# Inverting the scan's triangles by substitution on 16x16 blocks joined on TensorE, with two buffers for one stream of the preparation

## The chip, the cores and the metric

The kernel runs on one core of a Trainium2 chip. Times are device microseconds (us) of one execution. The metric is that time; lower is better. The engines are named as the profile names them: PE is TensorE, DVE is VectorE, ACT is ScalarE, POOL is GpSimd, SP is the engine that issues most of the loads.

## The reference

One layer of a bidirectional encoder, 1024 tokens of width 1024, all in float32: an FFN, a mixing layer (eight heads of banded attention beside eight heads of a two-way delta-rule scan), and a second FFN, each between norms and added to the stream. The change touches the scan alone:

```python
def _rwkv7_step(state, inp):
    r, w, k, v, kk, kka = inp
    sa = jnp.einsum('dbhvk,dbhk->dbhv', state, kk)
    state = state * w[..., None, :] - sa[..., :, None] * kka[..., None, :] + v[..., :, None] * k[..., None, :]
    y = jnp.einsum('dbhvk,dbhk->dbhv', state, r)
    return state, y
...
    _, ys = lax.scan(_rwkv7_step, state0, xs)      # 1024 steps, 2 directions, 8 heads of 64
    y = ys[:, :, 0] + jnp.flip(ys[:, :, 1], axis=1)
```

A step at a time would be 1024 steps in a row. The kernel computes 64 tokens (a chunk) at once. Within a chunk, each token's correction depends on those of the tokens before it, through a unit lower triangular 64x64 matrix, one for each chunk, direction and head. That matrix has to be inverted before the chunk's outputs and its final state can be had from matrix products.

## The kernel before

The program (`run`) goes through FFN 1, the input projection with the attention, the scan stage, the finish of the scan's output, the output projection and FFN 2. The scan stage takes 8 blocks of 2 chunks (`NB` = 8, `BLK` = 2, `C` = 64). One block has 2 chunks x 2 directions x 8 heads = 32 triangles. A block passes through four steps:

- `prep(n)` (L783) loads the block's streams for each direction: decay and rate (`th_w`, `th_a`, two buffers each) and one tile `in3` with r, k and kk (one buffer, so the second direction's load waits until the first direction's readers are through). DVE and ACT scale them, PE multiplies them (`lp`, L830), DVE masks the products into `lm` (L832), which holds the triangles. PE transposes `bk` into `bp` (L838). SP then writes the diagonal 32x32 blocks of `lm` to the scratch `x_d` in DRAM (4 DMAs, L846).
- `solve(n)` (L850) loads them back as `X`: 64 triangles of 32x32, each on two partitions that take alternate columns of the inverse. Two DVE operations a step (L866 multiplies, L868 subtracts) do the substitution in 31 steps into `Ti`. L870 copies `Ti` transposed, and POOL writes both to scratch (`t_d`, `tt_d`, 2 + 2 DMAs, L872 and L873).
- `merge(n)` (L875) loads the inverses of the diagonal blocks to where the products need them (`d11`, 2 DMAs, L883; `tt`, 4 DMAs, L886, all on POOL) and joins pairs of 32 to 64 by two products: `pa` (32 matmuls, L894), a copy on ACT (L896), `pb` (32 matmuls, L900), and a negated copy on ACT into `tt` (L902).
- `chain(n)` (L918) takes the block's two chunks in turn, each from the state `sv` that the one before left. PE: `xu` (L941); ACT copies it to `xs` (L944); PE: `xu` again, with the inverse `tt` as weights (L952, called the inverse product below); ACT copies to `uv`; PE: state and outputs `st`, `y` (L937, a helper's line); DVE scales the state into the next chunk's `sv` (L968).

Two more kinds of work lie between these on the same engines: the attended half of the output projection (`project_attended`: `po` L1064 and `yq` L1075 on PE, `yat` L1072 on DVE), which needs nothing of the scan, and the loads of `uv` and `sv` on POOL (`values`, L908).

What sets the order: the body of the loop calls merge(n), chain(n), and then prep and solve of block n+3, and a scheduler of the framework reorders the instructions of each engine by its own costs; on each engine they then run strictly in that order. Three sets of block buffers (`R0`, `R1`, `B0`) are used in turn, so prep(n+3) writes `lm` only where chain(n) has read it for the last time. A float32 matmul stands in the trace as two records, so 32 matmuls are 64 records.

Of the kernel before, what the change touches and what calls it, by code (L numbers as in the profile page):

```python
# [26 lines left out]
C, NC_, BLK = 64, 16, 2  # L27
TB = C * BLK
# [3 lines left out]
def _ap(src, off, pat):  # L32
    return bass.AP(tensor=src.tensor, offset=src.offset + off, ap=pat)
# [3 lines left out]
class _GateUp:  # L37
# [126 lines left out]
class _Kernel:  # L164
# [618 lines left out]
    def prep(self, n, p, psum, big):  # L783

        nc, V, A, T = self.nc, self.nc.vector, self.nc.scalar, self.nc.tensor
# [6 lines left out]
        for d in range(2):  # L792
# [48 lines left out]
            for k, v in (("pr", pt), ("bt", bt)):  # L841
                blk[k].append(v)
        for par in range(2):
            for k in range(2):
                r0 = par * 64 + k * 32
                self.nc.sync.dma_start(_ap(self.x_d[n % 4], (k * 2 + par) * 16 * 1024, [[32, 32], [1024, 16], [1, 32]]),  # L846
                                  lm[r0:r0 + 32, par, :, :, :, k * 32:k * 32 + 32].rearrange("p d i a t -> p (d i a) t"))
        return blk

    def solve(self, n, p):  # L850


        nc, V, G = self.nc, self.nc.vector, self.nc.gpsimd
        X = p.tile([128, 32, 32], F32, name="X", tag="X", bufs=2)
        for q in range(2):
            self.load(X[q * 64:q * 64 + 64].rearrange("p a b -> p (a b)"), self.x_d[n % 4])
        Ti = p.tile([128, 32, 16], F32, name="Ti", tag="Ti", bufs=2)
        tmp = p.tile([128, 144], F32, name="ttmp", tag="ttmp", bufs=2)
        tf = Ti.rearrange("p a b -> p (a b)")
        G.memset(tf, 0.0)  # L860
        for q in range(2):
            G.memset(tf[q * 64:q * 64 + 64, q * 16:512:33], 1.0)
        for s in range(31):
            r, m = 31 - s, s // 2 + 1
            tv = tmp[:, :r * m].rearrange("p (a b) -> p a b", a=r)
            V.tensor_tensor(tv, X[:, s, s + 1:][:, :, None].to_broadcast([128, r, m]),  # L866
                            Ti[:, s, 0:m][:, None, :].to_broadcast([128, r, m]), op=OP.mult)
            V.tensor_tensor(Ti[:, s + 1:, 0:m], Ti[:, s + 1:, 0:m], tv, op=OP.subtract)  # L868
        Tt = X[:, 0:16, :]
        V.tensor_copy(Tt, Ti.rearrange("p a b -> p b a"))  # L870
        for q in range(2):
            self.nc.gpsimd.dma_start(_ap(self.t_d[n % 4], q * 16, [[1024, 32], [32, 32], [1, 16]]), Ti[q * 64:q * 64 + 32])  # L872
            self.nc.gpsimd.dma_start(_ap(self.tt_d[n % 4], q * 32, [[1024, 64], [64, 16], [1, 32]]), Tt[q * 64:q * 64 + 64])  # L873

    def merge(self, n, blk, p, psum):  # L875

        nc, A, T = self.nc, self.nc.scalar, self.nc.tensor
# [3 lines left out]
        for par in range(2):  # L881
            o = par * 64
            self.nc.gpsimd.dma_start(d11[o:o + 32], _ap(self.t_d[n % 4], par * 16 * 1024, [[32, 32], [1024, 16], [1, 32]]))  # L883
            for k in range(2):
                r0 = o + k * 32
                self.nc.gpsimd.dma_start(tt[r0:r0 + 32, :, k * 32:k * 32 + 32],  # L886
                          _ap(self.tt_d[n % 4], (k * 2 + par) * 16 * 1024, [[32, 32], [1024, 16], [1, 32]]))
        pa = psum.tile([128, NI, 32], F32, name="pa", tag="mg")
        am = d11
# [5 lines left out]
        for lo, hi in lohi:  # L895
            A.copy(am[hi].rearrange("p i (c q) -> p i q c", q=2), pa[hi].rearrange("p i (q c) -> p i q c", q=2))  # L896
        pb = psum.tile([128, NI, 32], F32, name="pb", tag="mg")
# [201 lines left out]
    def constants(self):  # L1099
# [6 lines left out]
        for c, t in self.eps.items():  # L1106
# [16 lines left out]
        self.x_d, self.t_d, self.tt_d = ([self.dram(f"{n}{j}", [r, w]) for j in range(4)]  # L1123
                                         for n, r, w in (("x", 64, 1024), ("t", 32, 1024), ("tt", 64, 1024)))

# [31 lines left out]

    def scan_inverses(self, p):
        self.tt = [p.tile([128, 2 * BLK * 4, 64], F32, name=f"tt{j}") for j in range(2)]
        for t in self.tt:  # L1160
            self.nc.gpsimd.memset(t.rearrange("p a b -> p (a b)"), 0.0)

    def run(self):
        nc = self.nc
# [4 lines left out]
        with self.top as top:  # L1169
# [106 lines left out]
            self.scan_inverses(sc)  # L1276
            sc.tile([128, 112], F32, name="edge")
            s_eo, s_pe = ExitStack(), ExitStack()
# [157 lines left out]
```

## Time and profile before

| what | value |
|---|---|
| median of 3 runs | 2369.25 us (2357.99 to 2371.84) |
| the profiled execution's own time | 2369.46 us |
| its span in the trace | 2367.7 us |
| mean granted clock of TensorE in it | 0.96 |
| scan stage in it | about 1205 to 1590 us of the span |

How to read the rows further down. A row of the timeline has the start (us), the duration (us), the engine (an engine's name with a q is its DMA queue's issue), the line, the operation, output <- inputs, sizes, and how many records were drawn together; in brackets stands the idle time before it and what ended it. A row of groups has the count, then the busy time in us and the mean of one in ns, then the idle time ahead and its main causes. A row of stretches has start and end, length, then for PE, weight loads, DVE, ACT and POOL the busy us with the number of instructions, and last the granted clock of TensorE (1 is full), the busy share of the 16 DMA engines, and GB/s.

### The profile page before, as it was taken

Reading aid. Unit: us, or ns where it says so; the run is one execution under the profiler, and the core shown is the slowest. Engines: PE = TensorE matmul, PEld = TensorE weight load, DVE = VectorE, ACT = ScalarE, POOL = GpSimd, SP = SyncE. Lnnn points to the kernel's source line nnn. Section 1 sums busy time; section 2 is a strip of 40 time slices with the busy share of each in tenths; the row PEclk is TensorE's granted clock in tenths of the full one; section 3 lists DMA queues with packets and bytes.
Section 4 is the critical chain, followed back from the end, with each engine's and each line's share of the span. In section 5 each row is a group of like instructions: output and inputs, shape, how many; then the busy total and the mean of one; then the engine's idle time right before and its main releaser. Section 6 shows DMA issues by size and latency. Waiting matters only on the chain. (4 is left out here: it accounts for less than half of the span.)

```text
span 2367.7 us, 39507 instructions
## 1 busy us (share of the span) xinstructions
PE 2212.2 (93%) x14532; PEld 1784.9 (75%) x14532; DVE 1782.8 (75%) x2957; ACT 1034.4 (44%) x1958; POOL 608.7 (26%) x732
## 2 busy tenths in 40 slices
PE   6999999999999998999995889988799999999997
PEld 4788888878877676788774767765678888887886
DVE  8899999865676344667568767837889999987565
ACT  4322333354676413666545545445442333235453
POOL 6244443400000010111102242432334344441000
PEclk8999999999999998999996798989989999999999
DMA  5354445486652514322369676577534544447655
GB/s 156 107 174 151 170 146 170 167 266 193 220 185 98 193 42 134 91 81 71 94 161 223 165 183 176 151 208 256 178 95 168 174 167 154 169 153 265 195 188 181
DMA packets 359381, 386.04 MB, mean 163 GB/s; under 512 B 74258, under 2 KB 265618, under 8 KB 359188
## 3 DMA queue, kind: packets, MB, share of 16 engines
q1 hardware_dynamic: 308512, 276.43, 38.8%
q0 software_dynamic: 30320, 94.44, 11.3%
q10 hardware_dynamic: 20356, 12.66, 1.9%
q8 instruction: 114, 1.87, 0.3%
q14 instruction: 79, 0.65, 0.1%
HBM read 257.53 MB, written 125.89 MB: 162 GB/s over the span
## 5 line engine op out<-in xcount | busy, mean ns | idle before, releaser
L186 ACT ACTIVATE wh<-raw 128x512 fp32r<-128x512 f32 (+1 forms) x273 | 167.8, 626 | 264.1 <-DVE raw L62 95.0
L187 DVE TENSOR_TENSOR wl<-raw,wh 128x512 fp32r<-128x512 f32 (+1 forms) x273 | 277.6, 1020 | 3.1 <-ACT wh L186 2.0
L81 PE MATMUL gu<-xh,wh 128*128 128x512 f32 x704 | 277.9, 395 | 0.9 <-ACT xh L186 0.8
L81 PE MATMUL gu<-xl,wh 128*128 128x512 f32 x704 | 276.3, 393 | 0.0
L81 PE MATMUL gu<-xh,wl 128*128 128x512 f32 x704 | 276.2, 392 | 0.0
L415 PE MATMUL pd<-gl,gwh 128*128 128x512 f32 x616 | 240.4, 390 | 3.1 <-DVE gl L187 3.1
L415 PE MATMUL pd<-gh,gwh 128*128 128x512 f32 x616 | 239.6, 390 | 0.5 <-DVE row L86 0.5
L415 PE MATMUL pd<-gh,gwl 128*128 128x512 f32 x616 | 239.7, 389 | 0.0
L86 DVE TENSOR_TENSOR row<-gu,row 128x512 f32<-128x512 f32 x308 | 206.4, 682 | 23.2 <-PE gu L81 22.4
L187 DVE TENSOR_TENSOR gwl<-graw,gwh 128x512 fp32r<-128x512 f32 (+1 forms) x176 | 117.0, 667 | 129.7 <-ACT gwh L186 127.5
L116 POOL DMA_DIRECT2D d_hid<-row x154 | 84.7, 551 | 470.6 <-DVE row L114 444.2
L186 ACT ACTIVATE gwh<-graw 128x512 fp32r<-128x512 f32 (+1 forms) x176 | 101.4, 576 | 190.5 <-PE pd L415 162.2
L81 PEld LDWEIGHTS gu<-xh,wh 128*128 128x128 f32 x704 | 133.9, 190 | 29.5 <-ACT xh L186 2.0
L81 PEld LDWEIGHTS gu<-xl,wh 128*128 128x128 f32 x704 | 133.8, 190 | 27.9
L81 PEld LDWEIGHTS gu<-xh,wl 128*128 128x128 f32 x704 | 133.3, 189 | 27.5
L415 PEld LDWEIGHTS pd<-gl,gwh 128*128 128x128 f32 x616 | 115.6, 188 | 28.5 <-DVE gl L187 4.9
L415 PEld LDWEIGHTS pd<-gh,gwh 128*128 128x128 f32 x616 | 115.5, 188 | 25.6 <-DVE row L86 0.8
L415 PEld LDWEIGHTS pd<-gh,gwl 128*128 128x128 f32 x616 | 115.6, 188 | 23.8
L94 ACT ACTIVATE row<-row 128x512 f32<-128x512 f32 x44 | 27.9, 633 | 223.9 <-DVE row L86 216.4
L187 DVE TENSOR_TENSOR gl<-raw,gh 128x512 fp32r<-128x512 f32 x160 | 112.9, 717 | 15.7 <-ACT gh L186 15.4
L145 POOL TENSOR_TENSOR ws<-ws 128x512 f32<-128x512 f32 x88 | 114.4, 1300 | 1.2
L186 ACT ACTIVATE gh<-raw 128x512 fp32r<-128x512 f32 x160 | 98.0, 621 | 32.2 <-DMA raw<-in_ffn_w_down_dram 21.1
(356 smaller groups left out, 5353.4 us busy)
## 6 DMA issues: line engine op xcount, KB each, us to landing
d_hid<-row POOLq DMA_DIRECT2D x154, 256.0 KB, 2.5
graw<-d_hid SPq DMA_DIRECT2D x132, 256.0 KB, 3.0
raw<-in_ffn_w_gate_dram SPq DMA_DIRECT2D x88, 256.0 KB, 3.1
raw<-in_ffn_w_up_dram SPq DMA_DIRECT2D x88, 256.0 KB, 3.3
ws<-in_ffn_w_down_dram SPq DMA_DIRECT2D x88, 256.0 KB, 4.5
d_ws<-ws POOLq DMA_DIRECT2D x88, 256.0 KB, 2.3
raw<-d_ws SPq DMA_DIRECT2D x88, 256.0 KB, 2.7
raw<-in_ffn_w_down_dram SPq DMA_DIRECT2D x66, 256.0 KB, 3.3
```

The lines of the kernel that those rows point to most:

```text
L81: self.K.nc.tensor.matmul(ps, a[:, k, :], b[:, k, :], start=(k == 0 and i == 0), stop=(k == 3 and i == 2))
L86: add = lambda o, x: V.tensor_tensor(o, ps, x, op=OP.add)
L94: A.activation(y[:, 0], y[:, 0], AF.Silu)
L116: put = lambda n, y: G.dma_start(self.hid[n - 1, j // 2], y)
L145: G.tensor_tensor(o, a, b, op=OP.subtract)
L186: self.nc.scalar.activation(h, src, AF.Copy)
L187: (eng or self.nc.vector).tensor_tensor(l, src, h, op=OP.subtract)
L415: T.matmul(ps[x], a[:, ts], b, start=(m == 0 and k == 0), stop=(m == NM - 1 and k == 2))
```

## The change

Substitution now goes down to triangles of 16 only, and TensorE joins them to 32 before it joins 32 to 64 as before.

- `prep`: `in3` has two buffers. The diagonal blocks go to `x_d` as 16x16 blocks, in 8 DMAs.
- `solve`: one load. Each of the 128 partitions holds one whole 16x16 triangle (32 triangles x 4 diagonal blocks). 15 steps of two operations on at most 64 elements, one transposing copy of 256, and two contiguous writes.
- `merge`: 14 loads on POOL instead of 6, each 16 partitions x 16 x 16 (`tt` 8, `t0` 4, `d11` 2). New: product `p1` (64 matmuls of 32x32 weights and 16 columns), a copy on ACT that scales rows by -1 or 0 (`lower`), product `p2` (64 matmuls), product `p2b` for the transposed form (64 matmuls with 16-column weights), one DVE addition into `d11`, and 4 copies on ACT into `tt`. Then `pa` and `pb` as before. `d11`, `t0` and `p1` are now single tiles that last through the stage.
- once, in `scan_inverses`: clearing the new tiles and making `lower` with three small DVE operations.

```diff
-            x3 = p.tile([128, 3, 4, TB], F32, name="in3", tag="in3", bufs=1)
+            x3 = p.tile([128, 3, 4, TB], F32, name="in3", tag="in3", bufs=2)
...
-        for par in range(2):
-            for k in range(2):
-                r0 = par * 64 + k * 32
-                self.nc.sync.dma_start(_ap(self.x_d[n % 4], (k * 2 + par) * 16 * 1024, [[32, 32], [1024, 16], [1, 32]]),
-                                  lm[r0:r0 + 32, par, :, :, :, k * 32:k * 32 + 32].rearrange("p d i a t -> p (d i a) t"))
+        for q in range(8):
+            par, o = q // 4, q % 4 * 16
+            self.nc.sync.dma_start(_ap(self.x_d[n % 4], self.small(q), [[16, 16], [256, 16], [1, 16]]),
+                                   lm[par * 64 + o:par * 64 + o + 16, par, :, :, :, o:o + 16].rearrange(
+                                       "p d i a t -> p (d i a) t"))
...
+    def small(self, q):
+        return (q % 2 * 64 + q // 2 * 16) * 256
...
-        X = p.tile([128, 32, 32], F32, name="X", tag="X", bufs=2)
-        for q in range(2):
-            self.load(X[q * 64:q * 64 + 64].rearrange("p a b -> p (a b)"), self.x_d[n % 4])
+        X = p.tile([128, 16, 16], F32, name="X", tag="X", bufs=2)
+        self.load(X.rearrange("p a b -> p (a b)"), self.x_d[n % 4])
...
-        for s in range(31):
-            r, m = 31 - s, s // 2 + 1
+        for s in range(15):
+            r, m = 15 - s, s + 1
             tv = tmp[:, :r * m].rearrange("p (a b) -> p a b", a=r)
             V.tensor_tensor(tv, X[:, s, s + 1:][:, :, None].to_broadcast([128, r, m]),
                             Ti[:, s, 0:m][:, None, :].to_broadcast([128, r, m]), op=OP.mult)
             V.tensor_tensor(Ti[:, s + 1:, 0:m], Ti[:, s + 1:, 0:m], tv, op=OP.subtract)
...
-        for q in range(2):
-            self.nc.gpsimd.dma_start(_ap(self.t_d[n % 4], q * 16, [[1024, 32], [32, 32], [1, 16]]), Ti[q * 64:q * 64 + 32])
-            self.nc.gpsimd.dma_start(_ap(self.tt_d[n % 4], q * 32, [[1024, 64], [64, 16], [1, 32]]), Tt[q * 64:q * 64 + 64])
+        V.tensor_copy(X, Ti.rearrange("p a b -> p b a"))
+        self.nc.gpsimd.dma_start(self.t_d[n % 4], tf)
+        self.nc.gpsimd.dma_start(self.tt_d[n % 4], X.rearrange("p a b -> p (a b)"))
...
-        d11 = p.tile([128, NI, 32], F32, name="d11", tag="d11")
+        d11, t0, p1 = self.d11, self.t0, self.p1
...
+        block = lambda d, q: _ap(d[n % 4], self.small(q), [[16, 16], [256, 16], [1, 16]])
+        for q in range(8):
+            o = q * 16
+            if q % 2 == 0:
+                self.nc.gpsimd.dma_start(t0[o:o + 16], block(self.t_d, q))
+            elif q % 4 == 1:
+                self.nc.gpsimd.dma_start(d11[o:o + 16, :, 16:32], block(self.t_d, q))
+            c = o % 64
+            self.nc.gpsimd.dma_start(tt[o:o + 16, :, c:c + 16], block(self.tt_d, q))
+        quads = [(par, k, slice(par * 64 + k * 32, par * 64 + k * 32 + 32)) for k in range(2) for par in range(2)]
+        ps = psum.tile([128, NI, 16], F32, name="p1", tag="mg")
+        for j in range(NI):
+            d, i, pr = j // 8, j // 4 % 2, j % 4
+            for par, k, rs in quads:
+                T.matmul(ps[rs, j, :], lm[rs, par, d, i, pr, k * 32:k * 32 + 32], t0[rs, j, :], start=True, stop=True)
+        A.activation(p1, ps, AF.Copy, scale=self.lower)
+        ps = psum.tile([128, 2, NI, 16], F32, name="p2", tag="mg")
+        for j in range(NI):
+            for par, k, rs in quads:
+                T.matmul(ps[rs, 0, j, :], tt[rs, j, k * 32:k * 32 + 32], p1[rs, j, :], start=True, stop=True)
+        for j in range(NI):
+            for par, k, rs in quads:
+                T.matmul(ps[rs.start:rs.start + 16, 1, j, :], p1[rs, j, :], tt[rs, j, k * 32 + 16:k * 32 + 32],
+                         start=True, stop=True)
+        V.tensor_tensor(d11[:, :, 0:16], t0, ps[:, 0], op=OP.add)
+        for par, k, rs in quads:
+            o = rs.start
+            A.copy(tt[o:o + 16, :, k * 32 + 16:k * 32 + 32], ps[o:o + 16, 1])
```

Everything behind `pa` stays, 21 to 23 lines further down: in the changed kernel the operations of the substitution are L867 and L869, `p1` L895, `p2` L900, `p2b` L903, the addition L905, `pa` L915, `pb` L921, the state's scaling L989, the inverse product L973, `po` L1085.

The scheduler also orders the engines anew. On DVE, in the middle of the scan stage, the substitution of one block stood among the operations of the next block's prep (L810 to L832). `X`, `Ti` and `ttmp` are the tiles of solve, the tiles with `in_` are a direction's `in3`. Before:

```order
L866 TENSOR_TENSOR ttmp<-X,Ti 128x126
L868 TENSOR_TENSOR Ti<-Ti,ttmp 128x18x7
L1055 SCALAR_TENSOR_TENSOR wol<-wor,c_attn_out_g,woh 128x512
L866 TENSOR_TENSOR ttmp<-X,Ti 128x136
L832 TENSOR_TENSOR lm<-lp,k_tri 128x512
L868 TENSOR_TENSOR Ti<-Ti,ttmp 128x17x8
L832 TENSOR_TENSOR lm<-lp,k_tri 128x512
L866 TENSOR_TENSOR ttmp<-X,Ti 128x128
L832 TENSOR_TENSOR lm<-lp,k_tri 128x512
L868 TENSOR_TENSOR Ti<-Ti,ttmp 128x16x8
```

Now, in the same place (the substitution of block 2):

```order
L1093 TENSOR_TENSOR yat<-yat,rs 128x512
L867 TENSOR_TENSOR ttmp<-X,Ti 128x15
L869 TENSOR_TENSOR Ti<-Ti,ttmp 128x15
L867 TENSOR_TENSOR ttmp<-X,Ti 128x28
L869 TENSOR_TENSOR Ti<-Ti,ttmp 128x14x2
L867 TENSOR_TENSOR ttmp<-X,Ti 128x39
L869 TENSOR_TENSOR Ti<-Ti,ttmp 128x13x3
L867 TENSOR_TENSOR ttmp<-X,Ti 128x48
L869 TENSOR_TENSOR Ti<-Ti,ttmp 128x12x4
L867 TENSOR_TENSOR ttmp<-X,Ti 128x55
L869 TENSOR_TENSOR Ti<-Ti,ttmp 128x11x5
L905 TENSOR_TENSOR d_12027<-t_12028,p_13116 128x16x16
```

The substitution now runs in one piece, with the next blocks' preps ahead of it and behind it. The addition L905, the only DVE operation of a merge (here of block 0's), stands behind its sixth step.

On PE, around the merge of block 3, `pa` stood far ahead, and `pb` lay between the transposes of a prep. `lp` and `bp` belong to a prep, `xu`, `y` and `st` to the chain, `yq` and `po` to the output projection. Before:

```order
L830 MATMUL lp<-pr,bk 128x128 x16
L838 MATMUL bp<-ident,bk 128x64 x8
L900 MATMUL pb<-tt_12090,d_14043 32x32 x3
L838 MATMUL bp<-ident,bk 128x64 x8
L900 MATMUL pb<-tt_12090,d_14043 32x32 x29
L941 MATMUL xu<-sv,lm 64x64 x16
L937 MATMUL y<-pr,sv 64x64 x11
L952 MATMUL xu<-xs,tt_12090 64x64 x16
L1075 MATMUL yq<-ident,yat 128x128 x4
```

Now (`p_14496` is `p1`, `p_14562` holds `p2` and `p2b`):

```order
L838 MATMUL bp<-ident,bk 128x64 x8
L895 MATMUL p_14496<-t_12028,lm 32x16 x50
L958 MATMUL st<-sv,ident 64x256 x4
L958 MATMUL y<-pr,sv 64x64
L900 MATMUL p_14562<-p_12029,tt_12026 32x16 x64
L903 MATMUL p_14562<-tt_12026,p_12029 16x16 x64
L958 MATMUL y<-pr,sv 64x64 x15
L1096 MATMUL yq<-ident,yat 128x128 x4
L915 MATMUL pa<-d_12027,lm 32x32 x32
L962 MATMUL xu<-sv,lm 64x64
L1085 MATMUL po<-woh,yah 128x512
```

Both joins now stand behind the prep's products and in a row with the chain, with pieces of the chain (`st`, `y`) and of the output projection (`yq`, `po`) between one product and the next.

On POOL, the writes of block 3's substitution and the loads of its merge. Before:

```order
L872 DMA d_t_173<-Ti 1024x1x16
L873 DMA d_tt_185<-X 1024x1x32
L908 DMA sv<-d_vt 64x2x256 x2
L860 MEMSET Ti 128x512
L883 DMA d_14043<-d_t_173 32x16x32
L862 MEMSET Ti 64x16 x2
L886 DMA tt_12090<-d_tt_185 32x16x32 x2
L883 DMA d_14043<-d_t_173 32x16x32
L886 DMA tt_12090<-d_tt_185 32x16x32 x2
```

Now, directly behind the two writes L871 and L872:

```order
L929 DMA sv<-d_vt 64x2x256 x2
L862 MEMSET Ti 128x256
L863 MEMSET Ti 128x16
L929 DMA uv<-d_vt 64x2x256 x2
L888 DMA tt_12026<-d_tt_185 16x16x16 x2
L929 DMA sv<-d_vt 64x2x256 x2
L888 DMA tt_12026<-d_tt_185 16x16x16
L929 DMA uv<-d_vt 64x2x256 x2
L888 DMA tt_12026<-d_tt_185 16x16x16 x5
L884 DMA t_12028<-d_t_173 16x16x16 x3
L886 DMA d_12027<-d_t_173 16x16x16 x2
L884 DMA t_12028<-d_t_173 16x16x16
```

Ahead of the first list stands one more row of each write. There are now fewer writes and more loads, the loads of `uv` and `sv` lie among them, and the last load of `t0` stands behind the two of `d11`.

More of the change, by code (lines that the diff above doesn't have):

```diff
@@ L868, in solve @@
             V.tensor_tensor(Ti[:, s + 1:, 0:m], Ti[:, s + 1:, 0:m], tv, op=OP.subtract)
[L869 to L872, printed above, removed]
-            self.nc.gpsimd.dma_start(_ap(self.tt_d[n % 4], q * 32, [[1024, 64], [64, 16], [1, 32]]), Tt[q * 64:q * 64 + 64])
+        V.tensor_copy(X, Ti.rearrange("p a b -> p b a"))
@@ L875, in merge @@
+        self.nc.gpsimd.dma_start(self.t_d[n % 4], tf)
+        self.nc.gpsimd.dma_start(self.tt_d[n % 4], X.rearrange("p a b -> p (a b)"))
     def merge(self, n, blk, p, psum):
-        nc, A, T = self.nc, self.nc.scalar, self.nc.tensor
+        nc, A, V, T = self.nc, self.nc.scalar, self.nc.vector, self.nc.tensor
         NI, lm = 2 * BLK * 4, blk["lm"]
-        d11 = p.tile([128, NI, 32], F32, name="d11", tag="d11")
+        d11, t0, p1 = self.d11, self.t0, self.p1
         blk["tt"] = tt = self.tt[n % 2]
[L881 to L887, printed above, removed]
+        block = lambda d, q: _ap(d[n % 4], self.small(q), [[16, 16], [256, 16], [1, 16]])
@@ L895, in merge @@
         for lo, hi in lohi:
-            A.copy(am[hi].rearrange("p i (c q) -> p i q c", q=2), pa[hi].rearrange("p i (q c) -> p i q c", q=2))
+            A.copy(am[hi], pa[hi])
         pb = psum.tile([128, NI, 32], F32, name="pb", tag="mg")
@@ L1123, in constants @@
         self.x_d, self.t_d, self.tt_d = ([self.dram(f"{n}{j}", [r, w]) for j in range(4)]
-                                         for n, r, w in (("x", 64, 1024), ("t", 32, 1024), ("tt", 64, 1024)))
+                                         for n, r, w in (("x", 128, 256), ("t", 128, 256), ("tt", 128, 256)))
     def mix_columns(self):
@@ L1158, in scan_inverses @@
     def scan_inverses(self, p):
+        G, V = self.nc.gpsimd, self.nc.vector
         self.tt = [p.tile([128, 2 * BLK * 4, 64], F32, name=f"tt{j}") for j in range(2)]
-        for t in self.tt:
-            self.nc.gpsimd.memset(t.rearrange("p a b -> p (a b)"), 0.0)
+        self.d11 = p.tile([128, 2 * BLK * 4, 32], F32, name="d11")
+        self.t0, self.p1 = (p.tile([128, 2 * BLK * 4, 16], F32, name=n) for n in ("t0", "p1"))
+        for t in self.tt + [self.d11, self.t0]:
+            G.memset(t.rearrange("p a b -> p (a b)"), 0.0)
+        four = p.tile([128, 4], F32, name="four")
+        self.lower = p.tile([128, 1], F32, name="lower")
+        V.tensor_reduce(out=four, in_=self.ident.rearrange("p (a b c) -> p a b c", b=2, c=16)[:, :, 1], op=OP.add, axis=AX.X)
+        V.tensor_reduce(out=self.lower, in_=four, op=OP.add, axis=AX.X)
+        V.tensor_scalar(self.lower, self.lower, -1.0, None, op0=OP.mult)
     def run(self):
@@ L1276, in run @@
             self.scan_inverses(sc)
-            sc.tile([128, 112], F32, name="edge")
+            sc.tile([128, 96], F32, name="edge")
             s_eo, s_pe = ExitStack(), ExitStack()
```

6 lines of the change are left out of this document (3 added, 3 removed).

## The prediction

> **What bounds the kernel now.** I read the page's busy shares first, then the busy times by stretches of the scan stage, since the change touches nothing else, and then one line of the timeline that marks each block's progress. The page says PE first, DVE second:
>
> ```profile
> span 2367.7 us, 39507 instructions
> PE 2212.2 (93%) x14532; PEld 1784.9 (75%) x14532; DVE 1782.8 (75%) x2957; ACT 1034.4 (44%) x1958; POOL 608.7 (26%) x732
> ```
>
> That is an average over stages. The stretches are the start of the scan, the five block periods in which preps still run, and the two last blocks:
>
> ```profile
> 1205.00:1310.00 105.00, 76.90 (x637) 62.80 (x638) 80.29 (x210) 53.63 (x102) 17.24 (x28) 0.77 0.82 203
> 1310.00:1519.00 209.00, 185.02 (x2953) 151.94 (x2951) 157.87 (x459) 105.94 (x199) 63.21 (x105) 0.86 0.68 172
> 1519.00:1590.00 71.00, 61.12 (x1187) 49.29 (x1186) 30.61 (x93) 28.65 (x54) 32.60 (x43) 0.90 0.66 188
> ```
>
> In the middle PE is busy 89% of the time, but at a clock of 0.86, and DVE 76%. Neither is full, so something else sets the pace. The inverse product of a block's first chunk (L952) marks the blocks:
>
> ```profile
> 1310.40 1.15 PE L952 MATMUL xu<-xs,tt 64*64 64x64 f32 x32
> ...
> 1484.56 1.98 PE L952 MATMUL xu<-xs,tt 64*64 64x64 f32 x32 [0.68 <-ACT xs L944]
> 1519.14 1.15 PE L952 MATMUL xu<-xs,tt 64*64 64x64 f32 x32
> ...
> 1579.90 1.98 PE L952 MATMUL xu<-xs,tt 64*64 64x64 f32 x32
> ```
>
> Five periods take 1519.1 - 1310.4 = 208.7 us, 41.7 each; the last of them, with the least prep left, took 34.6. The two blocks behind them take 60.8. Now block 3's way from its triangles to its inverse:
>
> ```profile
> 1346.23 1.99 SPq L846 DMA_DIRECT2D d_x<-lm  x4
> ...
> 1365.88 0.19 DVE L866 TENSOR_TENSOR ttmp<-X,Ti 128x31 f32<-128x31 f32 x1 [2.77 <-DMA X<-d_x]
> ...
> 1400.39 0.60 DVE L870 COPY X<-Ti 128x512 f32<-128x512 f32 x1
> ...
> 1406.18 0.67 POOL L883 DMA_DIRECT2D d<-d_t  x1
> ...
> 1429.64 1.92 PE L894 MATMUL pa<-d,lm 32*32 32x32 f32 x64
> ...
> 1445.51 1.15 PE L952 MATMUL xu<-xs,tt 64*64 64x64 f32 x32
> ```
>
> From the write of the triangles to the inverse product pass 99 us. As the block buffers are three, chain n frees those of prep n+3, so prep, this way and the chain form a loop that goes round in three periods (125 us). The loop is the pace: no engine is full, and each waits for a piece of it. Its largest piece is the substitution, 35.1 us from 1365.9 to the end of the copy at 1401.0, of which its own operations are less than half:
>
> ```profile
> L866 DVE TENSOR_TENSOR ttmp<-X,Ti 128x126 f32<-128x126 f32 (+22 forms) x31 | 7.8, 252 | 3.5 <-DMA X<-d_x 2.8
> L868 DVE TENSOR_TENSOR Ti<-Ti,ttmp 128x126 f32<-128x126 f32 (+21 forms) x30 | 7.6, 255 | 0.7
> ```
>
> The 15.4 us of these stand in DVE's strict order among another block's prep, which takes the other 20.
>
> **The change, part by part.** *Substitution.* Narrow operations of the old one show what the new ones cost:
>
> ```profile
> 1528.26 0.19 DVE L866 TENSOR_TENSOR ttmp<-X,Ti 128x31 f32<-128x31 f32 x1 [3.33 <-DMA X<-d_x]
> ...
> 1546.89 0.23 DVE L866 TENSOR_TENSOR ttmp<-X,Ti 128x70 f32<-128x70 f32 x1
> 1547.16 0.23 DVE L868 TENSOR_TENSOR Ti<-Ti,ttmp 128x70 f32<-128x70 f32 x1
> ...
> 1548.41 0.19 DVE L866 TENSOR_TENSOR ttmp<-X,Ti 128x30 f32<-128x30 f32 x1
> ...
> 1549.07 0.17 DVE L868 TENSOR_TENSOR Ti<-Ti,ttmp 128x16 f32<-128x16 f32 x1
> 1549.28 0.60 DVE L870 COPY X<-Ti 128x512 f32<-128x512 f32 x1
> ```
>
> The 30 new operations have 15 to 64 elements, 45 in the mean: 30 x 0.20 = 6.0 us busy, 7.2 with the 0.04 us between two. The copy halves to 0.3. The last block's old one, with no prep beside it, took 21.6 us with its copy; a new one takes 14 less. In the middle DVE loses 9.7 us a block, and as the new operations stand in one piece, the way through the loop loses more: 35.1 falls to 7.5 where X is there in time, to some 15 where preps stand before it. I take 20 to 27 off the loop.
>
> *Products.* 192 matmuls are 384 records. Rows of the nearest form, 32 weights by 32 columns, at the full and at the half clock:
>
> ```profile
> 1388.22 1.20 PE L894 MATMUL pa<-d,lm 32*32 32x32 f32 x64
> 1429.64 1.92 PE L894 MATMUL pa<-d,lm 32*32 32x32 f32 x64
> ```
>
> 18.75 ns each and 30 ns each. The new ones have 16 columns: half of 18.75 if the columns set it, all of it if not. So 384 cost 3.6 to 7.2 us at the full clock, up to 11.5 at the half. I take 6, nearer to the row than to its half, as at so few columns what is fixed weighs more. [...]
>
> *The merge's other steps.* One copy on ACT of 128x256, one DVE addition, four narrow copies on ACT. The nearest rows, and those of the loads and writes on POOL:
>
> ```profile
> L896 ACT COPY d<-pa 32x512 f32<-32x512 f32 x16 | 9.9, 616 | 1.9 <-PE pa L894 1.7
> L970 ACT COPY yb<-y 128x256 f32<-128x256 f32 x30 | 9.7, 375 | 29.0 <-PE y L937 29.0
> L968 DVE TENSOR_TENSOR sv<-st,gc 64x512 f32<-64x512 f32 x30 | 20.6, 688 | 10.5 <-PE st L937 9.8
> ...
> L886 POOL DMA_DIRECT2D tt<-d_tt x32 | 20.6, 649 | 0.1
> L872 POOL DMA_DIRECT2D d_t<-Ti x16 | 13.6, 850 | 54.2 <-DVE Ti L868 24.7 <-DMA d_x<-lm 21.5 <-issue 8.0
> ```
>
> ACT gains 5 x 0.375 = 1.9 us a block and stands at 106 of 209 us: covered. The addition is at most 0.7 us on DVE, which got 9.7 back: covered. POOL issues 14 loads at 0.65 and 2 writes at 0.65 to 0.85 instead of 6 and 4: 3.1 to 3.5 us more, on POOL at 63 of 209 us, but in series in the loop. SP issues 3 more (8 + 1 for 4 + 2) at the row's 0.5 us: 1.5 us. All of it goes round the loop: 6 (products) + 0.4 + 0.7 + 1.5 (the merge's copies and addition) + 3.3 + 1.5 = 13.4 us. Against 20 to 27 less, the loop falls from 125 to between 111.4 and 118.4 us, 37.1 to 39.5 a period.
>
> *PE instead.* PE's 185.02 us in five periods are 37.0 a block; at the full clock they would be 37.0 x 0.86 = 31.8. With 6 more, 37.8. The merge's chain of products and copies hands over six times between PE and ACT or DVE, and most gaps hold `po`, `yq` or pieces of the chain; I take 1.7 us of gaps. So PE needs 39.5 us a period, as much as the loop at its slowest: PE takes over as the pace, and the gain stops there. This rests on the clock coming back when PE is nearly always busy. How it falls:
>
> ```profile
> 1416.40:1419.80 3.40, 0.12 (x2) 0.82 1.06 230
> 1419.80:1423.20 3.40, 1.21 (x8) 0.50 1.11 302
> 1423.20:1426.60 3.40, 3.40 (x22) 0.50 0.27 80
> ```
>
> (PE alone: busy, clock, DMA share, GB/s.) After a stretch of 3.4 us nearly without work PE gets half the clock, and keeps it through the next stretch though busy. The loop made such a pause; gaps of a copy's length, 0.4 to 0.7 us, are shorter.
>
> *Start and `in3`.* Until the first inverse product at 1310.4 the stage waits for merge 0 and the preps:
>
> ```profile
> 1286.36 0.31 PE L894 MATMUL pa<-d,lm 32*32 32x32 f32 x2 [8.84 <-DMA d<-d_t]
> 1297.39 1.91 PE L894 MATMUL pa<-d,lm 32*32 32x32 f32 x62
> DVE pr L810 <- DMA in<-d_rk: 5.5, 3, 3.5
> ```
>
> The second buffer of `in3` can save at most the 5.5 us that DVE waited for that tile in the whole stage. Three shorter substitutions save up to 29 us of DVE here, but merge 0's addition now stands behind six steps of block 2's substitution, and behind that block's prep and loads: I take 5 us of gain; the bounds are 0, if block 2 is as late as now, and 11, the time between the two `pa` rows. The last two blocks have no prep, 60.8 us with PE 61 of 71 busy: the substitution's end 14 us earlier matters little behind the products, 2 x 6 us of which come on top but fall into PE's idle and low-clock time. I take 3 us of gain, bounds 12 lost and 9 gained.
>
> *Sum.* 5 x (39.5 - 41.7) = -11, -5 at the start, -3 at the end: -19 on the profiled execution's 2369.46 us (its span is 1.8 less, and it stands at the median of 2369.25): 2350 us. The bounds of the terms alone, taken apart: start 0 to -11, end +12 to -9, the matmuls 3.6 to 7.2 us give 37.1 to 40.7 a period, -23 to -5.
>
> **Rivals.** *B, the loop stays the pace and PE is no limit.* PE's busy time counts matmuls in flight and the modelled ends, so work may close up. The last of the five periods, 34.6 us, shows that the chain, a merge and a part of the prep go through in that. If all reach it: 5 x (34.6 - 41.7) - 8 = -44: 2325 us. For it: DVE's work falls from 31.6 to about 22 a block. Against: that period had less prep on PE.
>
> *D, the products cost what the substitution saves.* At the half-clock row they take 11.5 us a block; or the clock stays at its 0.86, and PE's 37.8 us become 44.0 a period. 5 x (44.0 - 41.7) - 8 = +4: 2373 us, no change that can be told. For it: a clock of 0.77 to 0.90 in all three stretches, not just around one pause. Against: the row at 18.75 ns. [...]
>
> *C, slower: the merge's gaps starve PE.* Each merge now has three more round trips between PE and ACT or DVE, the addition waits in DVE's order behind substitution steps that wait for `X`, and PE's order puts prep products and chain behind the merge's. One pause of 3.4 us a merge halves the clock for the following stretches. It decides from a mean clock of 0.79, where PE's 37.8 become 48 a period; at 0.75 they become 50.4: 5 x (50.4 - 41.7) - 8 = +36, 2405 us. For it: the first stretch already stood at 0.77. Against: `po` and `yq`, which wait for nothing of the scan, fill the gaps in PE's order.
>
> *That the substitution stays stretched* because its operations wait for the prep's is the lower end of the loop's gain, and ends with D.
>
> **How the numbers follow.** The forecast, 2350 us with its own range of 2335 to 2366, gets 0.45; B 0.20; D 0.23; C 0.12. One per cent, 23.7 us, is about what a measurement of this kernel can tell from no change: faster is below 2345.6, slower above 2392.9. Faster: all of B and 0.18 of the forecast's lower part, 0.38. Slower: C and 0.01 of D, 0.13. The rest, 0.49, is within. The range leaves out C's 0.12 and 0.07 of B that goes beyond: 2318 to 2385 us.
>
> **What would show it.** Right: the substitution's operations (now L867, L869) in 7 to 15 us a block; the 192 new matmuls at 16 ns a record, some 6 us a block; the inverse product (now L973) every 39.5 us, PE busy over 94% there at a clock above 0.93. Wrong: periods near 35 us with PE idle (B); records of 25 to 30 ns or a clock of 0.86 (D); waits of PE for the merge's copies, its addition or its loads longer than 3.4 us, and a clock below 0.8 (C); a first inverse product later than 1310 us (the start).

## The result: 3.9% slower, and the profile after

| | before | changed |
|---|---|---|
| median | 2367.93 us (4 runs) | 2459.99 us (4 runs, 2457.02 to 2470.89) |
| ratio | 1 | 1.039, 95% interval 1.036 to 1.042 |
| span of the profiled execution | 2367.7 us | 2459.0 us |
| mean granted clock in it | 0.96 | 0.935 |

The forecast was 2350 us, with 2318 to 2385 as its range. The page of the changed kernel:

```profile
span 2459.0 us, 45571 instructions
...
PE 2286.4 (93%) x17604; PEld 1844.6 (75%) x17604; DVE 1721.9 (70%) x2712; ACT 1048.8 (43%) x1998; POOL 623.5 (25%) x774
```

DVE is 61 us less busy, as meant. PE is only 74 us more busy but ran 3072 more matmul records (8 blocks x 384). The stretches that answer to those before (up to the first inverse product, five periods, the last two blocks), and the 62 us behind the scan:

```profile
1205.00:1323.00 118.00, 83.88 (x1048) 67.50 (x1046) 78.93 (x191) 61.91 (x124) 26.96 (x49) 0.83 0.78 201
1323.00:1575.00 252.00, 221.41 (x4906) 182.86 (x4907) 120.77 (x308) 113.72 (x220) 73.27 (x133) 0.78 0.44 120
1575.00:1658.00 83.00, 70.97 (x1924) 60.23 (x1924) 9.05 (x16) 28.80 (x57) 17.28 (x30) 0.77 0.21 57
1658.00:1720.00 62.00, 45.55 (x218) 27.24 (x214) 29.52 (x51) 25.59 (x51) 18.03 (x14) 0.75 0.74 230
```

In the five periods DVE fell from 158 us of 209 to 121 of 252, and PE, 88% busy, ran at a clock of 0.78 instead of 0.86. Rows of the inverse product's line for the first chunks of blocks 0, 5 and 7:

```profile
1323.13 0.47 PE L973 MATMUL xu<-xs,tt 64*64 64x64 f32 x2 [1.21 <-ACT tt L923]
...
1574.51 1.68 PE L973 MATMUL xu<-xs,tt 64*64 64x64 f32 x30
...
1647.79 1.98 PE L973 MATMUL xu<-xs,tt 64*64 64x64 f32 x32 [0.68 <-ACT xs L965]
```

So the 91.3 us between the two spans fall in four places: 12.7 before the first inverse product (1323.1 against 1310.4), 42.7 in the five periods (251.4 against 208.7, 50.3 each instead of 41.7), 12.5 in the last two blocks (73.3 against 60.8), and 23.4 from there to the end (811.2 against 787.8), in code that the change doesn't touch.

The substitution did what was said. Its groups in the five periods, with the busy time and the mean of one:

```profile
L869 DVE TENSOR_TENSOR Ti<-Ti,ttmp 128x39 f32<-128x39 f32 (+7 forms) x78 | 16.1, 206 | 2.5
L867 DVE TENSOR_TENSOR ttmp<-X,Ti 128x39 f32<-128x39 f32 (+7 forms) x78 | 15.9, 204 | 3.6 <-DMA X<-d_x 1.3
...
L870 DVE COPY X<-Ti 128x256 f32<-128x256 f32 x5 | 1.9, 379 | 0.2
```

The 78 of each are 5.2 blocks of 15 steps, so 32.0 us are 6.2 a block, and the copy 0.38. The merge is another matter. PE's timeline of block 4's merge, from the last part of p1 to the inverse product that waits for it:

```profile
1506.82 1.12 PE L895 MATMUL p<-t,lm 32*32 32x16 f32 x100
...
1510.70 1.92 PE L900 MATMUL p<-p,tt 32*32 32x16 f32 x127 [0.66 <-ACT p L896]
...
1512.46 0.79 PE L903 MATMUL p<-tt,p 32*16 32x16 f32 x71
1514.76 0.65 PE L903 MATMUL p<-tt,p 32*16 32x16 f32 x55 [1.51 <-issue]
...
1518.28 1.92 PE L915 MATMUL pa<-d,lm 32*32 32x32 f32 x64
...
1522.54 1.92 PE L921 MATMUL pb<-tt,d 32*32 32x32 f32 x64
...
1528.21 1.15 PE L973 MATMUL xu<-xs,tt 64*64 64x64 f32 x32
```

From that part of p1 to the inverse product pass 21.4 us. Two things are to be seen: the hand-over of p1 (1507.9 to 1510.7 with its copy on ACT in it, filled with pieces of the chain up to 0.66 us), and a stop in the middle of p2b, 1.51 us, that nothing in the profile ends ("issue"). For most of the stretch PE is busy (18.3 us of the 20.5 from 1507.6), but at half the clock, 0.50, as the stretches further down show. What PE waited for, by line, in the changed kernel from 1323 to 1613 us (sum, times, longest):

```profile
PE p L903 <- issue: 12.8, 5, 3.3
PE p L900 <- issue: 4.5, 2, 2.5
...
PE lp L830 <- DVE lm L832: 2.4, 7, 0.7
```

and in the kernel before from 1310 to 1546 us:

```profile
PE lp L830 <- DVE lm L832: 11.9, 6, 5.5
...
PE pb L900 <- issue: 0.6, 1, 0.6
```

The wait for DVE that the change was to shorten fell from 11.9 to 2.4 us, and stops without a cause, which hardly stood there before, took its place. The clock beside such a merge (PE alone: busy, clock, DMA share, GB/s):

```profile
1502.00:1505.40 3.40, 2.74 (x42) 1.00 1.05 292
1505.40:1508.80 3.40, 3.20 (x132) 0.82 0.69 178
1508.80:1512.20 3.40, 2.74 (x119) 0.50 0.38 68
1512.20:1515.60 3.40, 1.89 (x165) 0.50 0.39 114
```

Every merge has such a stretch at half the clock, 6.8 to 34.1 us at 0.50, and here it lasts through pa, pb and the chain's first products. The 0.82 of the second row puts the fall 1.2 us before that row's end, at 1507.6 us, ahead of the stop in p2b. The 3.4 us up to that fall, and then those up to a fall in the kernel before, with the stretch behind it:

```profile
1504.20:1507.60 3.40, 2.95 (x128) 1.00 0.89 272
```

```profile
1476.60:1480.00 3.40, 2.79 (x77) 1.00 1.22 308
1480.00:1483.40 3.40, 3.33 (x92) 0.50 0.59 117
```

So the clock fell with PE over 80% busy, in the kernel before as well.

At the end, the finish stage's first load on SP. Before, 21.7 us ahead of block 7's inverse product, and in the changed kernel 12.4 us behind it:

```profile
1558.23 0.36 SPq L182 DMA_DIRECT2D g2w<-in_rwkv_g_dram  x1
```

```profile
1565.23 0.34 SPq L182 DMA_DIRECT2D X<-d_x  x1
1660.15 0.33 SPq L182 DMA_DIRECT2D g2w<-in_rwkv_g_dram  x1
```

SP stands still for 95 us. The waits of SP's queue name a `y` of the chain before (35.3 us) and an `st` of the chain now (94.5 us); by the two programs these are block 6's and block 7's. The tiles of the preparation's pool have become 2688 bytes per partition smaller (`X`, `Ti` and `ttmp` shrank by more than `in3` grew). The finish takes the memory that this pool and the first block buffer free, and now reaches into the second block buffer, which holds block 7.

### The profile page after: what moved, and what is told of

Read it like the earlier page. It is cut to its first block, busy times and chain, and to the rows that moved or that the text cites. A ratio compares the mean times of both kernels' runs of the same rounds, so it can differ in the third digit from the quotient of the medians.

```text
span 2459.0 us, 45571 instructions
## 1 busy us (share of the span) xinstructions
PE 2286.4 (93%) x17604; PEld 1844.6 (75%) x17604; DVE 1721.9 (70%) x2712; ACT 1048.8 (43%) x1998; POOL 623.5 (25%) x774
## 3 DMA queue, kind: packets, MB, share of 16 engines
q0 software_dynamic: 31856, 92.08, 10.2%
## 4 chain that ended last, share of the span: by engine, by line
PE 37%; DMA 5%; DVE 3%; issue 3%; ACT 2%; POOL 0%; SPq 0%; DVEq 0%; ACTq 0%; POOLq 0%
PE gu L81 16%; PE pd L415 8%; PE po L1085 2%; PE st L958 1%; PE y L958 1%; PE lp L830 1%; PE xu L962 1%; DMA th_a<-d_a 1%; DMA in<-d_rk 1%; PE xu L973 1%; PE pa L915 1%; DMA f_k<-d_kd 1%; PE pb L921 1%; PE p L900 0%; DMA wor<-in_w_out_dram 0%
```

## The experiments

Theories: **L**, the finish's memory lies on the last block's, which costs the 23 us at the end. **M**, the hand-overs of the longer merge stand in a row with the chain, and the gaps halve the clock (the forecast's rival C). **F**, PE runs out of instructions in dense runs of narrow matmuls, so they cost by their number. **N**, they cost by their busy time. **S**, the substitution, its loads or the new order cost it. (The expectation of the run without the join calls N "the number of matmuls"; from the run with the products made twice on, F stands for the number and N for the busy time, as here.)

### Room in the preparation's pool

```diff
             self.scan_constants(sp)
+            sp.tile([128, 672], F32, name="room")
```

> The changed kernel with 2688 bytes per partition left empty in the pool of the preparation, so that the finish stage's buffers come to lie on block 6's again and not on block 7's. Theory L (the late start of the finish costs about 24 us of the 92): 2432 to 2440 us, first finish load some 30 us before the last inverse product. Rival (the finish would have waited anyway, for PE or for y): 2455 to 2465 us.

2441.46 us, ratio to the kernel before 1.0329 (1.0309 to 1.0349): 18.5 us less than the changed kernel and just above theory L's range. The first load of the finish:

```profile
1621.59 0.33 SPq L182 DMA_DIRECT2D g2w<-in_rwkv_g_dram  x1
```

Block 7's inverse product stood at 1653.4 us, so the load is 31.8 us ahead of it again. From there to the end of the span, 2438.7 us, pass 785.3 us instead of 811.2: theory L holds for the end. Not all of it is won, since block 7 itself came 5.6 us later with the finish's work beside it.

### The join taken apart

First the join from 16 to 32 left out, from p1 to the copies:

```diff
-        ps = psum.tile([128, NI, 16], F32, name="p1", tag="mg")
...
-            A.copy(tt[o:o + 16, :, k * 32 + 16:k * 32 + 32], ps[o:o + 16, 1])
         pa = psum.tile([128, NI, 32], F32, name="pa", tag="mg")
```

> Leaves out the join from 16 to 32: the products p1, p2, p2b, their copies and the addition; loads, substitution and the join to 64 stay. Theories M (hand-overs of the merge in a row with the chain, and the half clock that follows), F (PE runs out of instructions in dense runs of small matmuls) and N (the number of matmuls) all expect the periods back at 35 to 41 us: 2385 to 2405 us, the finish still late. Rival S (the substitution, its loads or the new order cost it): still over 2435 us.

2352.09 us, 0.9952 (0.9934 to 0.9969), 108 us less than the changed kernel and more than any theory had it. Theory S falls: the substitution on 16, with all its loads, is no loss but a gain.

Then the hand-overs alone, with 12 wide products in place of 192 narrow ones:

```diff
-        for j in range(NI):
-            d, i, pr = j // 8, j // 4 % 2, j % 4
-            for par, k, rs in quads:
-                T.matmul(ps[rs, j, :], lm[rs, par, d, i, pr, k * 32:k * 32 + 32], t0[rs, j, :], start=True, stop=True)
+        for par, k, rs in quads:
+            T.matmul(ps[rs], lm[rs, par, 0, 0, 0, k * 32:k * 32 + 32], t0[rs], start=True, stop=True)
...
+            T.matmul(ps[rs, 0], tt[rs, 0, k * 32:k * 32 + 32], p1[rs], start=True, stop=True)
...
+            T.matmul(ps[rs.start:rs.start + 16, 1], p1[rs, 0, :], tt[rs, :, k * 32 + 16:k * 32 + 32],
+                     start=True, stop=True)
```

> The join's 192 matmuls of 16 columns become 12 of 256 columns, from the first triangle's weights alone (the other products are left out); copies, addition and their order of dependence stay. Theory M: most of the loss stays, 2440 to 2455 us. Theories F and N: near the kernel without the join, 2390 to 2410 us.

2377.62 us, 1.0040 (1.0019 to 1.0061), 25.5 us above the kernel without the join. That is below both expected ranges, as the kernel without the join was. So the hand-overs (with 12 products) cost a quarter of the loss, and theory M as the main cause falls.

And the 192 matmuls alone:

```diff
-        A.activation(p1, ps, AF.Copy, scale=self.lower)
...
-                T.matmul(ps[rs, 0, j, :], tt[rs, j, k * 32:k * 32 + 32], p1[rs, j, :], start=True, stop=True)
+                T.matmul(ps[rs, 0, j, :], tt[rs, j, k * 32:k * 32 + 32], t0[rs, j, :], start=True, stop=True)
...
-        V.tensor_tensor(d11[:, :, 0:16], t0, ps[:, 0], op=OP.add)
-        for par, k, rs in quads:
-            o = rs.start
-            A.copy(tt[o:o + 16, :, k * 32 + 16:k * 32 + 32], ps[o:o + 16, 1])
```

> All 192 matmuls of the join stay, but p2 and p2b read t0 and not p1, and the copies to p1 and tt and the addition are left out, so PE waits for no other engine within the join. Theory M: near the kernel without the join plus the matmuls' own 6 us a block, 2410 to 2430 us. Theories F and N: most of the loss stays, 2440 to 2455 us, with gaps in p2b that nothing in the profile ends.

2435.74 us, 1.0302 (1.0278 to 1.0327), 83.7 us above the kernel without the join, or 54 ns a matmul (83.7 / (8 x 192)). With the 25.5 of the hand-overs that makes 109, and the whole loss against the kernel without the join is 108. The matmuls are three quarters of it, though PE waits for another engine in them for 1.1 us in all. What stands in them, and ahead of `pa`, are stops that nothing in the profile ends: 14.7 + 4.1 + 8.7 us. The time lies between the two expected ranges.

### Busy time or number

p1 and p2b of the wide form are computed twice, by a loop `for again in range(2)` around each matmul of the two.

> As the run with 12 wide matmuls in place of the join's 192, but p1 and p2b are computed twice: 20 wide matmuls a block, whose busy time, about 38 us in all, is that of the 192 narrow ones (37.6 us in the changed kernel), with a tenth of the instructions. Theory F (the narrow ones cost by their number of instructions): 2380 to 2395 us. Theory N (they cost by their busy time): 2420 to 2450 us.

2371.67 us, 1.0028 (1.0006 to 1.0049). The three lines' busy time from 1300 to 1580 us was 14.8 + 5.8 + 10.3 = 30.9 us for 304 records, short of the 38 that were meant. The 12 wide ones had 22.2 us and took 2377.62 us, so 8.7 us more of busy time cost nothing; the 192 narrow ones, with 37.6 us from 1300 to 1660 us, took 2459.99:

```profile
L900 PE MATMUL p<-p,tt 32*32 32x16 f32 x1024 | 13.6, 192 | 19.7 <-ACT p L896 13.4 <-issue 6.2
L895 PE MATMUL p<-t,lm 32*32 32x16 f32 x896 | 12.2, 181 | 1.6 <-issue 1.6
L903 PE MATMUL p<-tt,p 32*16 32x16 f32 x1024 | 11.8, 186 | 18.7 <-issue 18.7
```

Theory N as the main cause falls. The stretch of the five periods in the kernel without the join, and in this one:

```profile
1310.00:1493.00 183.00, 170.43 (x2936) 140.26 (x2937) 113.64 (x288) 102.17 (x192) 73.32 (x135) 0.93 0.60 165
```

```profile
1316.00:1507.00 191.00, 182.37 (x3170) 141.61 (x3168) 116.37 (x282) 112.94 (x220) 73.86 (x135) 0.99 0.57 158
```

With wide products, hand-overs and all, PE is 95% busy at a clock of 0.99. That is what the forecast had for the change; the 192 narrow ones undid it.

### The same matmuls in the kernel before

Three runs add narrow matmuls ahead of `pa` in the kernel before, into a bank that nobody reads; 192 of 16 columns, 192 of 32, and 64 of 16:

```diff
+        px = psum.tile([128, NI, 16], F32, name="px", tag="mg")
+        for again in range(3):
+            for j in range(NI):
+                d, i, pr = j // 8, j // 4 % 2, j % 4
+                for par, k, rs in quads:
+                    T.matmul(px[rs, j, :], lm[rs, par, d, i, pr, k * 32:k * 32 + 32], tt[rs, j, k * 32:k * 32 + 16],
+                             start=True, stop=True)
         pa = psum.tile([128, NI, 32], F32, name="pa", tag="mg")
```

> The kernel before, with 192 matmuls of 32x32 weights and 16 columns ahead of pa in every merge, into a bank that nobody reads; no new copies, loads or hand-overs. Theory F (a narrow matmul costs by its instructions, whatever is around it): 2425 to 2455 us. Rival (the price lay in the changed kernel's order): 2367 to 2400 us.

2450.97 us, 1.0377 (1.0333 to 1.0421), 86.7 us above the kernel before, 56 ns a matmul.

> The same with 32 columns each, twice the columns. Theory F: within 10 us of the run with 16 columns. Theory N (columns count): 25 to 40 us more than that.

2446.03 us, 1.0346 (1.0298 to 1.0393). Twice the columns cost no more. They took no more of PE's time either, 39.7 us busy against 41.8, so this run speaks against a price by columns, not against one by busy time.

> The same with 64 matmuls of 16 columns instead of 192. If each one costs the same: a third of the 192's price, 2387 to 2397 us. Theory F with what PE holds in advance as a cover: less than a third, 2367 to 2382 us.

2394.75 us, 1.0139 (1.0096 to 1.0182), 30.5 us for a third of the matmuls, 60 ns each (44 to 84 by the interval). The price goes with the number, against the second expectation, but it isn't made of the same parts. In the trace of this run PE stood in the added products only once, and the clock of the five periods was not lower than before (0.86):

```profile
PE px L894 <- issue: 4.7, 1, 4.7
```

```profile
1314.00:1534.00 220.00, 198.13 (x3605) 162.23 (x3603) 159.58 (x460) 104.59 (x197) 64.75 (x108) 0.87 0.65 164
```

The added products were busy for 14.0 us; with the one stop that is 18.7 of the 22.4 us by which this span (2390.1) is longer. So at 64 most of the price is the matmuls' own time, and the stops are nearly all covered.

PE's timeline of one merge of the first of the three, with 192, shows what is added there:

```profile
1404.03 1.95 PE L894 MATMUL px<-tt,lm 32*32 32x16 f32 x171
1408.43 1.90 PE L894 MATMUL px<-tt,lm 32*32 32x16 f32 x128 [2.45 <-issue]
1415.19 0.63 PE L894 MATMUL px<-tt,lm 32*32 32x16 f32 x33 [4.86 <-issue]
```

PE goes through 128 records in 1.9 us and stops for 2.5 to 4.9. The profile names nothing that these products would wait for. The DMA view of the same 11.2 us has, among the queues with kind, packets, MB and share:

```profile
q8 instruction: 2, 0.03, 1.2%
```

Two packets of instructions, 16384 bytes each in the trace, for two stops: one from 1406.1 to 1407.0 us, one from 1412.6 to 1413.8. In the trace of this kernel all ten stops of `px` end 1.2 to 1.6 us after the end of such a packet, and so do the eleven stops without a cause in the changed kernel's three products. So PE was out of instructions there. Between the two stops lie exactly 128 matmul records and as many weight loads, 256 instructions. The totals fit one packet for as many: 35208 matmuls and weight loads stand against 139 of these packets in the changed kernel, 253 to a packet, and 29064 against 114 in the kernel before, 255. Here 256 were gone in 1.9 us, and the end of the next packet came 3.5 us after that.

```profile
PE px L894 <- issue: 29.8, 10, 4.9
```

Such stops are 29.8 of the 86.7 us, from 1300 to 1660 us, and the 192 matmuls' own busy time is 41.8 us, 5.2 a block. The clock in this kernel's five periods was 0.76 against 0.86, over 260 us; the share of time at half speed is twice what lacks to 1, so it went from 0.28 x 208.7 = 58 us to 0.48 x 260 = 125 us, and work done at half speed costs half of it: some 33 us (an estimate). The three together are more than 86.7, since the clock's part counts some of the matmuls' own time again and some of it all falls into waits that PE had before; the runs don't divide the price closer than this.

### The second buffer, and the order

`in3` back to one buffer, with the memory left empty, so that nothing moves:

```diff
-            x3 = p.tile([128, 3, 4, TB], F32, name="in3", tag="in3", bufs=2)
+            x3 = p.tile([128, 3, 4, TB], F32, name="in3", tag="in3", bufs=1)
...
+            sp.tile([128, 2208], F32, name="room")
```

> The changed kernel with in3 back at one buffer, and the freed 6144 bytes left empty beside the 2688, so that all buffers of the finish lie as in the run with room alone (2441 us). If the second buffer is worth something in the loop: 2446 to 2465 us. Rival: PE is the pace, the load is hidden either way, 2436 to 2446 us.

2444.38 us, 1.0328 (1.0293 to 1.0363), against 1.0329 with two: no gain from the second buffer can be told while PE is the pace. Whether it is worth something beside a join that costs less wasn't tried.

The merge of the next block written ahead of the chain, in the changed kernel with room and in the kernel before:

```diff
-                if n:
-                    self.merge(n, blk[n], sc, pm)
+                if n + 1 < NB:
+                    self.merge(n + 1, blk[n + 1], sc, pm)
                 self.chain(n, blk.pop(n), sc, pc)
```

> The changed kernel with the room in the preparation's pool, and merge(n+1) written ahead of chain(n), so that the scheduler can lay the join between the pieces of the chain before. Theory M: the hand-overs are covered, 2370 to 2400 us. Theory F: PE still has the same instructions to fetch, stalls and half clock stay for the most part, 2405 to 2435 us. Beside it stands the same without the new order, 2441 us.

2403.68 us, 1.0133 (1.0098 to 1.0167), 37.8 us less than with room alone. It lies on the edge between the two expectations. In the profiled execution (2388.85 us, the fastest of the four and some 15 us under the others) the stops in p2b stayed (18.3 us in 8 of them), but the five periods took 206.8 us instead of the 247.8 with room alone, at a clock of 0.90: the early merge hides much of what the join holds up.

> The kernel before with merge(n+1) written ahead of chain(n). If the hand-overs of the merge cost something before too: 2345 to 2360 us. If its products stood well already: 2360 to 2375 us.

2370.40 us, 0.9994 (0.9969 to 1.0019): no difference, as expected if the merge's two products already stood well in the kernel before.

### Both edits without the join, and the join with half the matmuls

The kernel without the join, with the room:

> Leaves out the join from 16 to 32 (p1, p2, p2b, copies, addition), with the 2688 bytes of room in the preparation's pool. The two effects add up if they are two: 2352 - 24 = 2325 to 2335 us. If the finish is held by something else once the scan is short: 2345 to 2355 us.

2342.56 us, 0.9905 (0.9878 to 0.9932), between the two expectations. Room won 9.5 us here and 18.5 in the changed kernel. From block 7's inverse product to the end of the span it was 22.1 us less (787.4 for 809.5), but that product came 10.0 us later (1550.4 for 1540.4), with the finish's work now ahead of it.

Last, the whole join with 96 matmuls. The core of it:

```diff
+            self.nc.gpsimd.memset(tt[o:o + 32, :, 32:64], 0.0)
...
+        for j in range(NI):
+            d, i, pr = j // 8, j // 4 % 2, j % 4
+            for par, hs in halves:
+                T.matmul(ps[hs, j, :], lm[hs, par, d, i, pr, 0:64], t0[hs, j, :], start=True, stop=True)
...
+                A.activation(p1[rs], ps[rs, :, k * 16:k * 16 + 16], AF.Copy, scale=self.lower[rs])
...
+                T.matmul(ps[lo, j, 0:16], tt[lo, j, 0:32], p1[lo, j, :], start=True, stop=True)
...
+                T.matmul(ps[hs.start + 32:hs.start + 48, j, :].rearrange("p (k c) -> p k c", k=2), p1[hs, j, :],
+                         tt[hs, j, :].rearrange("p (k c) -> p k c", k=2)[:, :, 16:32], start=True, stop=True)
```

> The whole join, with 96 matmuls instead of 192: p1 takes both quarters of a half at once (64x64 weights against t0 laid out in blocks, 32 columns), p2 is made only where it is read, p2b takes both quarters at once. Copies and additions are one more each way (8 copies on ACT for 5, 2 additions for 1); POOL clears a corner of tt. t0 and p1 lie in the preparation's pool, so the finish lies as in the run with room (2441 us). Theory F at the 57 ns a matmul of the dead matmuls in the kernel before: 96 x 8 x 57 ns = 44 us less, 2390 to 2405 us. Theory M (the hand-overs): 2430 to 2450 us.

2391.85 us, 1.0103 (1.0078 to 1.0128), 49.6 us less than with room and 192 matmuls, in spite of three more copies on ACT and one more addition. Half of the 98.9 us that lie between the join of 192 with room and no join with room (2342.56) is 49.5, so the price goes with the number of matmuls in the real join too, though these also have other shapes. The stops without a cause in its products are down to 5.4 us in 2 of them.

> The same with merge(n+1) written ahead of chain(n). Theory F: 44 us less than the 2404 us of the early merge with 192 matmuls, 2352 to 2370 us. Theory M: the hand-overs were covered there already and one more copy and addition changes nothing, 2395 to 2410 us.

2375.50 us, 1.0029 (1.0011 to 1.0047), 28 us less than the early merge with 192, less than the 44 expected, and between the two expected ranges. The join's three products have no stops without a cause left. No version with the whole join was faster than the kernel before, and against that kernel this one loses at the start: its first inverse product comes at 1324.3 us, 13.9 later. The five periods take 203.5 us, 5.2 less, and the 13.6 us by which the last two blocks are shorter (47.2) are lost again behind them (801.1 us to the end of the span, 13.3 more). Why start and end are longer wasn't followed further.

## Why the prediction was wrong, point by point

- **What bounds the kernel before**: right as far as the runs show. With the substitution cut and no join behind it, the five periods fell to 183.3 us (1310.0 to 1493.3), 36.7 each, which fits a loop, not an engine, as the pace.
- **Substitution**: right. 6.2 us and 0.38 a block for the forecast 6.0 and 0.3.
- **Products**: this step failed. "384 cost 3.6 to 7.2 us at the full clock ... I take 6" priced a narrow matmul by its own time alone. For that time it was right: the 192 dead matmuls were busy for 41.8 us in 8 blocks, 5.2 a block. But 192 cost 82 to 87 us in 8 blocks, 10.2 to 10.8 us a block. PE runs out of instructions in them and stands, 29.8 us in the run with dead ones, for which the sum has no term, and more of the work around them runs at half the clock (the mean of the five periods there is 0.76, before 0.86). The upper end at the half clock, 11.5, held the number by luck. The rows show 100 records in 1.12 us, 127 in 1.92 at a clock of 0.50, and 128 in 1.90 ahead of a stop of 4.86.
- **PE instead, with the clock back at 1**: failed with it. PE was 88% busy in the five periods, but its clock fell to 0.78. The stops, 13 us in p2b alone from 1323 to 1613 us, the hand-overs and the half clock make the period 50.3 instead of 39.5. With wide products in place of the narrow ones the same hand-overs left the clock at 0.99.
- **How the clock falls**: "after a stretch of 3.4 us nearly without work" was too lenient. In the rows above it fell behind stretches in which PE was busy for 2.95 us of 3.4, and for 2.79 in the kernel before.
- **The merge's other steps**: "covered" was wrong by size. The hand-overs, with the 12 wide products in them, cost some 25 us, 3 us a block.
- **Start**: 5 us of gain were taken, 12.7 were lost. Without the join the first inverse product came at 1310.0 us, and with 192 dead matmuls in the kernel before at 1323.4, so the products alone can make the loss. The addition's place on DVE isn't it: with the addition kept and 12 wide products it came at 1315.6. `in3` gave nothing that can be told.
- **The end**: 3 us of gain were taken, 12.5 were lost in the last two blocks.
- **Not in the sum at all**: the 23.4 us behind the scan. The smaller tiles moved the finish's memory onto the last block's. Only the work that the change issues was counted, not where its tiles come to lie.
- **Rival C** had the sign and the half clock (0.78, and it decided from 0.79), but not the cause: the hand-overs between engines are a quarter of the join's cost. It had 2405 us.

## What to carry to other kernels

Before many small matmuls take over work from another engine, price them by their number: here a float32 matmul with 32x32 weights cost 53 to 60 ns of the kernel's time, of which its own busy time was about half (26 to 27 ns), whether of 16 or 32 columns, and whether its result was used or not. With 12 wide matmuls in place of the 192 (other products, the same hand-overs) the join cost 25 us instead of 108. A change of tile sizes also moves what is allocated later: see which buffers the next stage's first loads wait for, on both sides of the change. And a forecast that counts on the full clock has to ask for pauses: here PE was 88% busy in the five periods at a clock of 0.78, and 95% busy without stops at 0.99.

## What the hardware showed

- PE ran out of instructions. In a dense run of 32x16 matmuls it did 128 records (with their weight loads 256 instructions) in 1.9 us, and it stood for 2.45 and 4.86 us, until 1.4 us after the end of a packet of 16384 bytes of instructions. The second of the two packets began 2.3 us after its stop had begun, the first 0.1 us; why wasn't tried. With 64 such matmuls a merge instead of 192 it stood in them once from 1300 to 1660 us.
- In the traces of both kernels the granted clock is 1 or 0.50, and each stretch at one of the two lasts 3.41 us or a multiple of that (the last is cut off by the end). It went to half behind stretches of 3.4 us in which PE was busy for 2.95 us, and for 2.79 in the kernel before, so neither the stops nor the join's narrow matmuls are needed for it. With 64 narrow matmuls a merge and one stop the clock of the five periods was 0.87, against 0.86 before; with 192 and the stops it was 0.76. How much of that fall is the stops' own these runs don't tell apart.
